# One-instruction seed of 1/sqrt, and a last FFN bank, output included, cut into smaller columns

## The chip, the cores and the metric

The kernel runs on one core of a Trainium2 chip. The metric is the device time of one execution in microseconds (us); each version is executed several times and the median is compared. The engines are named as in the profile: PE (TensorE, matmul), DVE (VectorE), ACT (ScalarE), POOL (GpSimd), SP (SyncE, which here issues most DMAs).

## The reference, cut to what matters

Two transformer-like blocks run one after the other on 256 tokens of width 1024, all in float32: first RWKV mixing, block attention, cross attention and a mixture of 32 experts, then retention with pooling, a SwiGLU feed-forward layer (FFN), a convolution layer and a second FFN. The change touches the norm that stands ahead of every layer and the very end:

```python
def rms_norm(x, g):
    x32 = x.astype(jnp.float32)
    y = x32 * lax.rsqrt(jnp.mean(x32 * x32, axis=-1, keepdims=True) + EPS)
    return (y * g).astype(x.dtype)
...
    h = h + swiglu(rms_norm(h, ffn_norm_g[layer]), ffn_w_gate[layer], ffn_w_up[layer], ffn_w_down[layer])
return rms_norm(h, final_norm_g)
```

## The kernel before, in words

Tokens lie on the 128 partitions in two groups, `tt` = 0 (tokens 0 to 127) and `tt` = 1 (tokens 128 to 255); the residual stream `x` is a tile of 128 x 2 x 1024. Where a row of 1024 columns is made by matmuls it goes to two PSUM banks of 512 columns, `c` = 0 and 1, so that `py[c][tt]` are four banks. A float32 product is made as three matmuls of split operands (lines 467 to 469 of `out_rows`): high by high, low by high, high by low.

`rsqrt` (line 223) makes 1/sqrt(x) on DVE without a table: an integer shift right by one (line 226), an integer multiply by -1 and add of a constant (line 227), which together are the well known seed, then three Newton steps. For at most two columns a step is lines 235 and 238 on one column each, with -x/2 made once (line 231). Fifteen calls are made in the whole kernel: in the norms, in the head norms of RWKV and retention, in the router and in the convolution layer.

`ffn(1)` is the last layer. It leaves its last two chunks of the down projection to `last`, as two functions: `before(c, tt)` adds the second to last chunk to bank `py[c][tt]` (six matmuls of 512 columns), `products(c, tt)` the last one (six more).

`last` (line 287) ends the kernel. `add(c, tt)` issues the last products, adds the bank to `x` (DVE, line 2299), squares and sums the half row (ACT, line 2301, an ACTIVATE and the read of its accumulator into `ss`) and multiplies by the gain (POOL, line 2303) for the halves that need it. `store(tt)` adds the two partial sums (line 2307), calls `rsqrt`, scales the two halves and sends each to DRAM with a DMA of 256 KB (line 2318): for `tt` = 1 the first half is scaled by DVE (line 2314) and sent from SP's queue, the second by ACT (line 2312) and sent from ACT's own queue.

In a `manual_schedule` block each engine runs its instructions in the order in which the code issues them. `last` is such a block, with this order:

```python
with self.tc.manual_schedule(engines={PE, ACT, DVE, POOL}):
    before(0, 0)
    before(1, 0)
    before(0, 1)
    add(0, 0)
    add(1, 0)
    store(0)
    before(1, 1)
    add(0, 1)
    add(1, 1)
    store(1)
```

Elsewhere, outside such blocks, a planner with a model of costs sets each engine's order when the kernel is built. So the splitting of weights (`wlo`, line 323, on DVE) can come to stand between two steps of an `rsqrt`.

Of the kernel before, what the change touches and what calls it, by code (L numbers as in the profile page):

```python
# [10 lines left out]
I32 = mybir.dt.int32  # L11
AF = mybir.ActivationFunctionType
OP = mybir.AluOpType
# [150 lines left out]
class Block:  # L164
# [37 lines left out]
    def vectors(self, pool, first, last):  # L202
        self.vec_at, b = VEC[first][0], VEC[last][1]
        self.vec = pool.tile([128, b - self.vec_at], F32, name="vec", tag="vec")
        return self.vec, self.i["vec"][:, self.vec_at:b]
# [17 lines left out]
    def rsqrt(self, out, x):  # L223
        nc = self.nc
        tmp = self.small(x.shape[-1], name="rs")
        nc.vector.tensor_scalar(out.bitcast(I32), x.bitcast(I32), 1, None, op0=OP.logical_shift_right)
        nc.vector.tensor_scalar(out.bitcast(I32), out.bitcast(I32), -1.0, float(0x5f3759df),
                                op0=OP.mult, op1=OP.add)
        if x.shape[-1] <= 2:
            half = self.small(2, name="rx")[:, 0:x.shape[-1]]  # L230
            nc.vector.tensor_scalar(half, x, -0.5, None, op0=OP.mult)
            for _ in range(3):
                for n in range(x.shape[-1]):
                    t, y = tmp[:, n:n + 1], out[:, n:n + 1]
                    nc.vector.scalar_tensor_tensor(t, y, y, half[:, n:n + 1], op0=OP.mult, op1=OP.mult)
                for n in range(x.shape[-1]):
                    t, y = tmp[:, n:n + 1], out[:, n:n + 1]
                    nc.vector.scalar_tensor_tensor(y, t, 1.5, y, op0=OP.add, op1=OP.mult)
            return
        for _ in range(3):  # L240
            nc.vector.tensor_tensor(tmp, out, out, op=OP.mult)
            nc.vector.scalar_tensor_tensor(tmp, tmp, -0.5, x, op0=OP.mult, op1=OP.mult)
            nc.vector.scalar_tensor_tensor(out, tmp, 1.5, out, op0=OP.add, op1=OP.mult)
# [896 lines left out]
    def cross(self):  # L1140
        nc, i, c = self.nc, self.i, self.c
        self.marks = [self.loads[n].ins for n in (-6, -4)]
        last, end = self.los[-3].ins, self.los[-1].ins
        with self.tc.issue_after(self.loads[-4].ins):
            gm, gx = self.gains(i["mem_norm"], i["norm_xattn"])
# [25 lines left out]

        with self.tc.manual_schedule(engines={PE, ACT, DVE, POOL}):
            rs = self.rstd(m, after=last)
            with self.tc.issue_after(end):
                self.scaled(m, rs, gm, m)
# [732 lines left out]
    def ffn(self, layer, beside=iter(())):  # L1908

        nc, i = self.nc, self.i  # L1910
        wg, wu, wd = [i[n][layer] for n in ("ffn_w_gate_2", "ffn_w_up_2", "ffn_w_down_2")]
        gain, = self.gains(i["ffn_norm_g_2"][layer])
        cut = lambda w, f: w[:, f * 256:(f + 1) * 256].rearrange("(k p) c -> p k c", p=128)
        h, p0, w1, rs = self.enter(gain, cut(wg, 0), cut(wu, 0), self.t9 if layer else self.tx, self.tx)
        r = self.gr.tile([128, 256], F32, name="r", tag="r")
        rb = r[:, None].to_broadcast([128, 2, 256])
        py = [[self.bank(f"f{tt}{c}", self.py) for tt in range(2)] for c in range(2)]
        n = FF // 256
        half = lambda c: slice(c * 512, (c + 1) * 512)
        rows = lambda f: self.weights(wd[f * 256:(f + 1) * 256].rearrange("(k p) c -> p k c", p=128))  # L1920
        cols = lambda w, f: self.weights(cut(w, f))

        def total(w, to):
            ps = [self.bank("f2").rearrange("p (m t) -> p m t", m=2) for _ in range(2)]
            self.out_cols2(w, ps)
            for cb in range(2):
                nc.scalar.activation(to[:, cb], ps[cb][:, 0], AF.Copy)
                nc.vector.tensor_tensor(to[:, cb], to[:, cb], ps[cb][:, 1], op=OP.add)

        def down(f, a):  # L1930
            w = rows(f)
            for c in range(2):
                self.out_rows(w, a, py[c], first=(f == 0), last=False, cols=half(c))

        prev = None
        for f in range(n):
            s = self.pr.tile([128, 512], F32, name="fs", tag="pr").rearrange("p (a t) -> p a t", a=2)
            pg = p0
            if f:
                pg = s  # L1940
                total(cols(wg, f), s)
            pu = self.pr.tile([128, 512], F32, name="fu", tag="pr").rearrange("p (a t) -> p a t", a=2)
            total(cols(wu, f) if f else w1, pu)
            if f == 0:
                self.along(rs, r)
            nc.vector.tensor_tensor(s, pg, rb, op=OP.mult)
            nc.scalar.activation(s, s, AF.Silu)  # L1947
            scaled = nc.gpsimd.tensor_tensor(s, s, rb, op=OP.mult)  # L1948
            if f > 1:
                with self.tc.issue_after(scaled.ins):  # L1950
                    next(beside, None)
            nc.vector.tensor_tensor(s, s, pu, op=OP.mult)
            if f < n - 1:
                a = self.ffa.tile([128, 2, 2, 256], F32R, name="fa", tag="fa")
            else:
                a = self.big(F32R, "fa")[:, 0:1024].rearrange("p (m k t) -> p m k t", m=2, k=2)
            self.split(s, a[:, 0], a[:, 1])
            if f == n - 1 and layer:
                w2, a2 = rows(f - 1), prev[1]
            elif prev is not None:  # L1960
                down(*prev)
            prev = (f, (a[:, 0], a[:, 1]))
        w = rows(n - 1)

        def products(c, tt):
            self.out_rows(w, prev[1], py[c], first=False, cols=half(c), tokens=(tt,))

        def before(c, tt):
            self.out_rows(w2, a2, py[c], first=False, last=False, cols=half(c), tokens=(tt,))

        self.left = (before, products, py) if layer else (products, py, False)

    def conv_weights(self):
# [313 lines left out]
    def last(self):  # L2287
        nc, x = self.nc, self.x
        before, products, py = self.left
        g, = self.gains(self.i["final_norm_g_2"])  # L2290
        xg = self.beside("xg").rearrange("p (a d) -> p a d", a=2)
        o = self.big(name="out", room=self.tx).rearrange("p (a d) -> p a d", a=2)
        half = lambda c: slice(c * 512, (c + 1) * 512)
        ss = self.small(4, name="ss").rearrange("p (t c) -> p t c", t=2)

        def add(c, tt):
            xs = x[:, tt, half(c)]
            products(c, tt)
            nc.vector.tensor_tensor(xs, xs, py[c][tt], op=OP.add)
            sq = self.sq.tile([128, 512], F32, name="sq", tag=f"sq{c}")  # L2300
            nc.scalar.activation(sq, xs, AF.Square, scale=1.0 / 32, accum_out=ss[:, tt, c:c + 1])
            if c or not tt:
                nc.gpsimd.tensor_tensor(xg[:, tt, half(c)], xs, g[:, half(c)], op=OP.mult)

        def store(tt):
            ms, rs = self.small(1, name="ms"), self.small(1, name="rstd")
            nc.vector.tensor_scalar(ms, ss[:, tt, 0:1], ss[:, tt, 1:2], 1e-6, op0=OP.add, op1=OP.add)
            self.rsqrt(rs, ms)
            for c in range(2):
                to, xs = o[:, tt, half(c)], xg[:, tt, half(c)]  # L2310
                if c:
                    nc.scalar.activation(to, xs, AF.Copy, scale=rs)
                elif tt:
                    nc.vector.scalar_tensor_tensor(to, x[:, tt, half(c)], rs, g[:, half(c)], op0=OP.mult, op1=OP.mult)
                else:
                    nc.gpsimd.tensor_scalar(to, xs, rs, None, op0=OP.mult)
                queue = nc.scalar if c and tt else nc.sync
                queue.dma_start(out=self.out[tt * 128:(tt + 1) * 128, half(c)], in_=to)

        with self.tc.manual_schedule(engines={PE, ACT, DVE, POOL}):  # L2320
            before(0, 0)
# [4 lines that stand above are left out]
            store(0)  # L2326
            before(1, 1)
            add(0, 1)
            add(1, 1)
            store(1)  # L2330


# [22 lines left out]
```

## Time and profile before

| what | value |
|---|---|
| median of 3 runs | 1380.73 us (1380.12 to 1380.96) |
| the profiled execution's own time | 1378.72 us |
| its span, first to last instruction | 1376.8 us |
| busy: PE, DVE, ACT, POOL | 89%, 56%, 39%, 11% of the span |
| granted TensorE clock, mean | 0.929 of full speed |
| DMA | 360.10 MB, mean 262 GB/s |

The profile records one execution. All times below are counted from the start of its span, which is 1.92 us shorter than the execution's own time; that time is 2.01 us under the median of the runs. "Idle before" is how long an engine stood still ahead of an instruction, with the instruction whose end released it.

### The profile page before, as it was taken

How to read it: one execution, taken by the hardware profiler on the slowest of the kernel's cores; microseconds unless marked ns; L12 is line 12 of the kernel's file. 1: busy time of each engine (PE TensorE's matmuls, PEld its weight loads, DVE VectorE, ACT ScalarE, POOL GpSimd, SP SyncE). 2: the span in 40 equal slices, each digit the busy share in tenths (PEclk: the TensorE clock that was granted, in tenths of full speed). 3: DMA queues.
4: the chain of work that ended last, by engine and by line, in shares of the span. 5: the costliest groups of instructions: out<-in, count | busy, mean ns of one | idle time of the engine just before them, and what ended most of it. 6: DMA issues, size and time to landing. Idle time of an engine off the chain costs nothing.

```text
span 1376.8 us, 28610 instructions
## 1 busy us (share of the span) xinstructions
PE 1230.7 (89%) x12204; PEld 1023.2 (74%) x12204; DVE 769.3 (56%) x1559; ACT 539.6 (39%) x884; POOL 147.0 (11%) x124
## 2 busy tenths in 40 slices
PE   8999999999886777676767699999999999999997
PEld 7989888898765455444535499788888997888886
DVE  5577547876332132131212386877776789766665
ACT  4553533554221111121111274354555535555553
POOL 1022201002000000000000032012221200111112
PEclk9999989999997877888868799999999999999999
DMA  7535513996999999999999998365556268665520
GB/s 213 184 115 158 159 40 128 356 411 253 385 417 416 418 418 420 418 419 418 419 419 418 381 301 292 102 230 184 184 192 190 78 162 266 207 195 195 191 77 31
DMA packets 146455, 360.10 MB, mean 262 GB/s; under 512 B 6672, under 2 KB 101904, under 8 KB 121744
## 3 DMA queue, kind: packets, MB, share of 16 engines
q1 hardware_dynamic: 144800, 353.69, 69.5%
q0 software_dynamic: 1376, 4.25, 1.0%
q8 instruction: 97, 1.59, 0.5%
q14 instruction: 38, 0.31, 0.1%
q10 hardware_dynamic: 144, 0.26, 0.0%
HBM read 354.92 MB, written 3.26 MB: 260 GB/s over the span
## 4 chain that ended last, share of the span: by engine, by line
PE 41%; DMA 24%; DVE 3%; ACT 1%; issue 0%; SPq 0%; ACTq 0%; DVEq 0%
PE f L445 11%; DMA raw<-in_w_exp_down_dram 10%; DMA raw<-in_w_exp_gate_dram 7%; DMA raw<-in_w_exp_up_dram 6%; PE f L446 6%; PE f L468 3%; PE f L467 3%; PE f L469 3%; PE cv L2105 2%; PE first L452 1%; PE v L469 1%; PE v L467 1%; PE v L468 1%; PE gu L1576 1%; PE xe L1545 1%; PE r L468 1%
## 5 line engine op out<-in xcount | busy, mean ns | idle before, releaser
L323 DVE TENSOR_TENSOR wlo<-raw,whi 128x1024 fp32r<-128x1024 f32 x231 | 292.4, 1273 | 151.8 <-ACT whi L321 146.5
L321 ACT ACTIVATE whi<-raw 128x1024 fp32r<-128x1024 f32 x238 | 249.9, 1057 | 220.5 <-PE f L445 87.7
L445 PE MATMUL f<-hT,whi 128*128 128x512 f32 x672 | 236.3, 395 | 0.0
L1576 PE MATMUL gu<-raw,xe 128*32 128x128 f32 x4096 | 168.9, 312 | 53.5 <-DMA raw<-in_w_exp_up_dram 33.4
L1576 PEld LDWEIGHTS gu<-raw,xe 128*32 128x32 f32 x4096 | 130.9, 122 | 92.2 <-DMA raw<-in_w_exp_up_dram 43.4
L446 PE MATMUL f<-hT,wlo 128*128 128x256 f32 x672 | 188.4, 280 | 0.0
L445 PEld LDWEIGHTS f<-hT,whi 128*128 128x128 f32 x672 | 126.0, 188 | 29.4
L1600 DVE SCALAR_TENSOR_TENSOR ye<-dn,gs,ye 32x256 fp32r<-32x256 f32 x128 | 61.5, 481 | 134.5 <-ACT ye L1599 133.8
L1599 ACT ACTIVATE ye<-dn,gs 32x256 fp32r<-32x256 f32 x128 | 59.6, 465 | 174.8 <-PE dn L1591 118.3
L446 PEld LDWEIGHTS f<-hT,wlo 128*128 128x128 f32 x672 | 127.0, 189 | 0.8
L1591 PE MATMUL dn<-raw,ht 128*32 128x256 f32 x1024 | 85.1, 460 | 45.3 <-DMA raw<-in_w_exp_down_dram 37.7
L1591 PEld LDWEIGHTS dn<-raw,ht 128*32 128x32 f32 x1024 | 34.2, 124 | 82.2 <-DMA raw<-in_w_exp_down_dram 29.6
L1658 DVE SCALAR_TENSOR_TENSOR hd<-gu,scale,hd 128x128 f32<-128x128 f32 x32 | 11.2, 350 | 106.6 <-ACT hd L1657 106.5
L1657 ACT ACTIVATE hd<-gu,scale 128x128 f32<-128x128 f32 x32 | 11.8, 367 | 149.8 <-PE gu L1576 149.8
L1948 POOL TENSOR_TENSOR fs<-fs,r 128x512 f32<-128x512 f32 x22 | 39.3, 1787 | 290.0 <-ACT fs L1947 290.0
L467 PE MATMUL f<-whi,fa 128*128 128x512 f32 x176 | 69.3, 394 | 0.0
L468 PE MATMUL f<-whi,fa 128*128 128x512 f32 x176 | 69.0, 392 | 0.2 <-DVE fa L342 0.2
L469 PE MATMUL f<-wlo,fa 128*128 128x512 f32 x176 | 68.7, 390 | 0.0
L1545 PEld LDWEIGHTS xe<-oh,xn 128*128 128x128 f32 x256 | 36.8, 231 | 12.9 <-issue 12.1
L1545 PE MATMUL xe<-oh,xn 128*128 128x128 f32 x256 | 39.0, 320 | 6.5 <-PEq L1669 5.7
L429 PE MATMUL gt<-hT,whi 128*128 128x256 f32 x128 | 38.7, 303 | 0.0
L467 PEld LDWEIGHTS f<-whi,fa 128*128 128x128 f32 x176 | 33.1, 188 | 7.6 <-ACT fa L341 0.5
(618 smaller groups left out, 2547.3 us busy)
## 6 DMA issues: line engine op xcount, KB each, us to landing
raw<-in_w_exp_gate_dram SPq DMA_DIRECT2D x64, 1024.0 KB, 19.9
raw<-in_w_exp_up_dram SPq DMA_DIRECT2D x64, 1024.0 KB, 19.9
raw<-in_w_exp_down_dram SPq DMA_DIRECT2D x63, 1024.0 KB, 20.0
raw<-in_ffn_w_gate_dram SPq DMA_DIRECT2D x22, 1024.0 KB, 5.4
raw<-in_ffn_w_up_dram SPq DMA_DIRECT2D x22, 1024.0 KB, 5.3
raw<-in_ffn_w_down_dram SPq DMA_DIRECT2D x22, 1024.0 KB, 4.8
raw<-in_w_in_dram SPq DMA_DIRECT2D x20, 1024.0 KB, 5.3
raw<-in_conv_w_pw_dram SPq DMA_DIRECT2D x12, 1024.0 KB, 5.5
```

The source lines that it names most:

```text
L321: nc.scalar.activation(hi, raw[:, k:k + step], AF.Copy)
L323: self.los.append(eng.tensor_tensor(lo, raw[:, k:k + step], hi.bitcast(F32), op=OP.subtract))
L445: nc.tensor.matmul(ps[cb], lhsT=whi[:, k, s], rhs=self.two[n][:, :, kk], start=f, stop=False)
L446: nc.tensor.matmul(ps[cb][:, 1], lhsT=wlo[:, k, s], rhs=self.two[n][:, 0, kk], start=False, stop=l)
L467: nc.tensor.matmul(ps[tt], lhsT=hi[:, k0 + k, s], rhs=whi[:, k, cols], start=f, stop=False)
L468: nc.tensor.matmul(ps[tt], lhsT=lo[:, k0 + k, s], rhs=whi[:, k, cols], start=False, stop=False)
L469: nc.tensor.matmul(ps[tt], lhsT=hi[:, k0 + k, s], rhs=wlo[:, k, cols], start=False, stop=l)
L1545: nc.tensor.matmul(ps[:, a], lhsT=xn[:, tt, d * 128:(d + 1) * 128], rhs=oh[:, tt].rearrange("p e s -> p (e s)"), start=(tt == 0), stop=(tt ...
L1576: nc.tensor.matmul(pg[quarter(n), at:at + 128], lhsT=xe[:, 4 * kh + k], rhs=w[:, k, n // 2, n % 2], start=(at == kh == k == 0), stop=(at > ...
L1591: nc.tensor.matmul(pd[n % 2][quarter(n), 0:256], lhsT=ht[:, quarter(2 * half + k)], rhs=wd[:, k, n * 256:(n + 1) * 256], start=(half + k = ...
L1599: nc.scalar.activation(hi, part, AF.Copy, scale=gs[q])
L1600: nc.vector.scalar_tensor_tensor(lo, part, gs[q], hi.bitcast(F32), op0=OP.mult, op1=OP.subtract)
```

## The change

Four edits:

- In `rsqrt` the shift and the multiply-add become one instruction: the integer bits times -0.5 plus the same constant. It holds for all fifteen calls.
- The last products, bank `py[1][1]`, are issued in two parts of 256 columns. Part 0 goes on in `py[1][1]`; part 1 starts a fresh bank, `f3`. DVE adds the whole of `py[1][1]` to `x` after part 0, and `f3` to the last 256 columns after part 1.
- The half row's square is also made in two parts. As there are now three partial sums, DVE adds the first two in an instruction of its own, issued between part 0's square and part 1's add.
- The output of the last 128 tokens is scaled and sent in quarters of 256 columns (128 KB): columns 0 and 256 on DVE, 512 and 768 on ACT; the first three are sent from SP's queue, the fourth from ACT's.

```diff
     def rsqrt(self, out, x):
-        nc.vector.tensor_scalar(out.bitcast(I32), x.bitcast(I32), 1, None, op0=OP.logical_shift_right)
-        nc.vector.tensor_scalar(out.bitcast(I32), out.bitcast(I32), -1.0, float(0x5f3759df),
-                                op0=OP.mult, op1=OP.add)
+        nc.vector.tensor_scalar(out.bitcast(I32), x.bitcast(I32), -0.5, float(0x5f3759df), op0=OP.mult, op1=OP.add)
...
-        def products(c, tt):
-            self.out_rows(w, prev[1], py[c], first=False, cols=half(c), tokens=(tt,))
+        def products(c, tt, cut=slice(0, 512), to=None):
+            self.out_rows(w, prev[1], [to, to] if to is not None else py[c], first=cut.start > 0,
+                          cols=slice(c * 512 + cut.start, c * 512 + cut.stop), tokens=(tt,))
...
-        def add(c, tt):
-            xs = x[:, tt, half(c)]
-            products(c, tt)
-            nc.vector.tensor_tensor(xs, xs, py[c][tt], op=OP.add)
+        def add(c, tt, part=None):
+            cut = slice(part * 256, part * 256 + 256) if part is not None else slice(0, 512)
+            at = slice(c * 512 + cut.start, c * 512 + cut.stop)
+            xs = x[:, tt, at]
+            to = self.bank("f3")[:, 0:256] if part else py[c][tt][:, cut]
+            products(c, tt, cut, to)
+            if part == 0:
+                nc.vector.tensor_tensor(x[:, tt, half(c)], x[:, tt, half(c)], py[c][tt], op=OP.add)
+            else:
+                nc.vector.tensor_tensor(xs, xs, to, op=OP.add)
             sq = self.sq.tile([128, 512], F32, name="sq", tag=f"sq{c}")
-            nc.scalar.activation(sq, xs, AF.Square, scale=1.0 / 32, accum_out=ss[:, tt, c:c + 1])
+            n = c + (part or 0)
+            nc.scalar.activation(sq[:, cut], xs, AF.Square, scale=1.0 / 32, accum_out=ss[:, tt, n:n + 1])
+            if part == 0:
+                nc.vector.tensor_tensor(ss[:, tt, 1:2], ss[:, tt, 0:1], ss[:, tt, 1:2], op=OP.add)
             if c or not tt:
-                nc.gpsimd.tensor_tensor(xg[:, tt, half(c)], xs, g[:, half(c)], op=OP.mult)
+                nc.gpsimd.tensor_tensor(xg[:, tt, at], xs, g[:, at], op=OP.mult)
...
             self.rsqrt(rs, ms)
+            if tt:
+                quarters(rs)
+                return
...
+        def quarters(rs):
+            for n, at in enumerate((0, 512, 256, 768)):
+                s = slice(at, at + 256)
+                to = o[:, 1, s]
+                if n % 2:
+                    nc.scalar.activation(to, xg[:, 1, s], AF.Copy, scale=rs)
+                else:
+                    nc.vector.scalar_tensor_tensor(to, x[:, 1, s], rs, g[:, s], op0=OP.mult, op1=OP.mult)
+                queue = nc.scalar if n == 3 else nc.sync
+                queue.dma_start(out=self.out[128:256, s], in_=to)
...
             add(0, 1)
-            add(1, 1)
+            add(1, 1, 0)
+            add(1, 1, 1)
             store(1)
```

## Rows read from the trace of the kernel before

**Rows 1.** The page: busy time with share and instructions of each engine.

```profile
PE 1230.7 (89%) x12204; PEld 1023.2 (74%) x12204; DVE 769.3 (56%) x1559; ACT 539.6 (39%) x884; POOL 147.0 (11%) x124
```

**Rows 2.** Stretches: length, busy us per engine, granted clock, DMA share, GB/s.

```profile
0.00:30.00 30.00, 24.95 (x153) 23.05 (x154) 16.49 (x43) 14.43 (x23) 3.32 (x13) 0.89 0.80 242
...
375.00:434.00 59.00, 43.97 (x768) 30.88 (x768) 19.01 (x58) 13.96 (x31) 0.00 (x0) 0.86 1.01 418
...
900.00:1000.00 100.00, 100.00 (x537) 85.98 (x536) 71.88 (x98) 51.73 (x74) 19.00 (x11) 1.00 0.60 194
```

**Rows 3.** The chain that ended last, two stretches: start, length, what.

```profile
814.10 0.12 PE q L430
...
1364.03 0.24 PE f L469
...
1369.17 0.73 ACT sq L2301 x2
...
1372.02 0.72 ACT out L2312
```

**Rows 4.** Timeline of PE: its last matmul.

```profile
1367.96 0.39 PE L469 MATMUL f<-wlo,fa 128*128 128x512 f32 x1
```

**Rows 5.** Timeline of DVE from the first `store` to the end.

```profile
1366.03 0.15 DVE L226 TENSOR_SCALAR rstd<-ms 128x1 int32<-128x1 int32 x1
1366.21 0.15 DVE L227 TENSOR_SCALAR rstd<-rstd 128x1 int32<-128x1 int32 x1
1366.29 0.15 DVE L231 TENSOR_SCALAR rx<-ms 128x1 f32<-128x1 f32 x1
...
1367.70 1.38 DVE L2299 TENSOR_TENSOR x<-x,f 128x512 f32<-128x512 f32 x2
1369.92 0.21 DVE L2307 TENSOR_SCALAR ms<-ss 128x1 f32<-128x1 f32 x1 [0.85 <-ACT sq L2301]
...
1371.95 0.75 DVE L2314 SCALAR_TENSOR_TENSOR out<-x,rstd,raw 128x512 f32<-128x512 f32 x1
```

**Rows 6.** Groups by line and shape, ACT and DVE: busy us, mean ns, idle before.

```profile
L2081 ACT ACTIVATE csg<-csg,vec 128x256 f32<-128x256 f32 x6 | 2.7, 503 | 19.9 <-DVE csg L2078 19.9
L2022 ACT ACTIVATE csq<-dw 128x256 f32<-128x256 f32 x6 | 2.5, 417 | 0.2
...
L1928 DVE TENSOR_TENSOR fu<-fu,f 128x256 f32<-128x256 f32 x22 | 9.1, 414 | 0.0
L2085 DVE SCALAR_TENSOR_TENSOR ut<-cat,vec,csg 128x256 f32<-128x256 f32 x6 | 2.6, 480 | 0.0
```

**Rows 7.** Timeline: the last two DMA issues, on SP's and ACT's queue.

```profile
1372.73 0.33 SPq L2318 DMA_DIRECT2D out_dram<-out  x1
1372.77 0.37 ACTq L2318 DMA_DIRECT2D out_dram<-out  x1
```

**Rows 8.** DMA issues by tile: KB each, median us from issue to landing.

```profile
away<-ut SPq DMA_DIRECT2D x6, 144.0 KB, 1.9
out_dram<-out SPq DMA_DIRECT2D x3, 256.0 KB, 2.3
...
out_dram<-out ACTq DMA_DIRECT2D x1, 256.0 KB, 2.7
```

**Rows 9.** Timeline of DVE: line 227, first and last of 15 calls.

```profile
9.27 0.17 DVE L227 TENSOR_SCALAR rstd<-rstd 128x2 int32<-128x2 int32 x1
...
1370.36 0.15 DVE L227 TENSOR_SCALAR rstd<-rstd 128x1 int32<-128x1 int32 x1
```

**Rows 10.** Tile `rstd`: one of those that waited for it (us, times).

```profile
  PE tr L509: 3.3, 1
```

**Rows 11.** Timeline of DVE: one planned call, weights between its two seed steps.

```profile
223.78 0.17 DVE L226 TENSOR_SCALAR rs<-var 128x8 int32<-128x8 int32 x1
224.58 1.23 DVE L336 TENSOR_TENSOR wlo<-raw,whi 128x1024 fp32r<-128x1024 f32 x1 [0.63 <-ACT whi L335]
225.73 0.17 DVE L227 TENSOR_SCALAR rs<-rs 128x8 int32<-128x8 int32 x1
```

## What I expect of it, before it is run

> **What bounds the kernel now.** I read the page first [rows 1]: PE is busy for 89% of the span, so a DVE instruction taken out counts only where PE, or the end of the kernel, waits for DVE. Then the stretches [rows 2]. From 375 us to about 800 the DMA engines are full (share 1.01, 418 GB/s) while PE is busy for 43.97 of 59 us: the expert weights set the pace there. In the stretch from 900 to 1000 us PE is busy for 100.00 of 100, and the chain at 814 us runs through PE [rows 3]: PE sets the pace after the experts. Only then the end. PE's last matmul starts at 1367.96 [rows 4], yet the span goes on to 1376.8, and in these 8 us the chain goes ACT, DVE, ACT [rows 3]. So the tail is a chain on DVE and ACT, then a DMA.
>
> The reader is to see one thing in the timeline of DVE [rows 5]. When PE ends, DVE is late: it has just done the first `store`'s 1/sqrt, and its two adds for tokens 128 to 255 run back to back, 1367.70 to 1369.08, the second after its bank is complete. A bank that is complete sooner in its first half is therefore of no use by itself; PE is not what the adds wait for.
>
> **The change part by part.** I count the tail from DVE's instructions, against the profiled execution (1378.72 us, 2.01 under the median of the runs).
>
> *Seed in the first `store`.* One step goes: line 227 starts 0.18 us after line 226 [rows 5] (1366.21 less 1366.03). DVE then goes straight on to the adds, which are ready to run: -0.18 us.
>
> *Bank in two parts, on PE.* Twelve matmuls of 256 columns stand for six of 512. A 256-column one takes a step of 0.12 us in the chain at 814 us, a 512-column one 0.24 [rows 3], so PE ends where it did, at about 1368.35 (1367.96 plus 0.39) [rows 4]. DVE asks for the last part over a microsecond later (below). Cost nothing; without that cover it would be what PE is late by.
>
> *The wait that is added.* Before, DVE's last add ends at 1369.08, ACT's square starts at 1369.17 (0.09 later) and takes 0.73 with its read-out [rows 3], and DVE goes on 0.02 later, at 1369.92 [rows 5]: 0.84 us from add to sum. After, the add of part 0 is as long as the old one (it covers all 512 columns), so it ends where the old last add did, less 0.18. Then comes the instruction that adds two partial sums. It needs part 0's square from ACT, and DVE runs in order, so the add of part 1 queues behind it; for that add ACT's second square waits, and for that the end. A half square takes 0.73 less 0.22, the difference between a scaled copy of 512 columns (0.72) [rows 3] and an ACT instruction of 256 with a per-partition operand (0.503) [rows 6]: 0.51. So after part 0's add: 0.09 + 0.51 + 0.02 to the sum; 0.08 until the next, independent instruction starts (1366.29 less 1366.21, rows 5; the upper bound is a dependent step, 0.18); 0.41 for the add of 256 columns [rows 6]; 0.09 + 0.51 + 0.02 again. That makes 1.73 us for 0.84: +0.89, at most +0.99. The lower bound is the case that the second add isn't held: 0.41 + 0.09 + 0.51 + 0.02 = 1.03, or +0.19. I take +0.89, as the sequence in the code leaves no choice to DVE. The part 1 add would start about 0.70 after 1368.90, at 1369.6, so PE's 1368.35 is covered by 1.2 us. That a bare square of 256 columns takes 0.417 [rows 6], 0.09 under the scaled one, moves nothing, since the read-out is in the 0.73. POOL's product with the gain is cut likewise; no step of the chain comes from POOL.
>
> *Seed in the second `store`.* The same step on the path: -0.18.
>
> *Output in quarters.* Counted from DVE's first scaling, at 1371.95 before [rows 5]. Before: DVE is done at 0.75, the DMAs are issued at 0.78 (SP) and 0.82 (ACT) [rows 7], and the one on ACT's queue takes 2.7 to land [rows 8]: 3.52. After: DVE's two take 0.48 each [rows 6], done at 0.48 and 0.96; ACT starts 0.07 later (1372.02) [rows 3] and with 0.503 each is done at 0.57 and 1.07. SP has three issues where it had one, in the order of columns 0, 512, 256: at 0.51, 0.87 and 1.23, each some 0.36 after the one ahead (0.33 and 0.37) [rows 7]; the third finds its data ready since 0.96, so it waits for SP alone. ACT's own follows at 1.10. The nearest row for a quarter (128 KB, 1 KB per partition) is a store of 144 KB from SP, `away`, which lands in 1.9 us [rows 8]: the last quarter lands at 1.23 + 1.9 = 3.13, ACT's perhaps 0.05 later. I take 3.17: -0.35. Bounds: -0.39 (3.13), 0 if a quarter takes the 2.3 of a half on SP (3.53), +0.41 at the 2.7 of ACT's.
>
> Here the Trainium skill speaks against the cut. "DMA: Bandwidth & Descriptors", section "Anatomy of one DMA", gives a DMA a fixed 2.0 us plus its bytes at 436 GB/s, in a fit for DMAs issued from GpSimd; 128 KB would take an estimated 2.3 us and the -0.35 would become about 0. The 1.9 us of the row is less than this formula's fixed part and its bytes together, so the row stands against the page for this size; what quarters of one output do is in no row here.
>
> *The other thirteen seeds.* Each saves about 0.2 us on DVE; calls run from 9 to 1370 us [rows 9]. Six lie after 375 us, and PE or the DMA stream covers them as the stretches show [rows 2]. Seven lie before. One has a visible waiter on PE, the transposes at the start [rows 10]; but of 0.2 us won there little can be left after the stretch in which the weights' bytes set the pace. Bounds: 0, and 7 x 0.2 = -1.4. I take -0.1, near to nothing, as a single wait of that kind is seen and the full DMA stretch lies behind it.
>
> Sum: -0.18 + 0.89 - 0.18 - 0.35 - 0.1 = +0.08 us. On the profiled execution 1378.8, on the median of the runs 1380.8 us.
>
> **The rivals.** About 0.2%, or 2.8 us, is what a measurement of this kernel can tell from no change.
>
> Faster, by *early seeds that carry through*: all seven savings ahead of 375 us reach the end. For it speaks the wait at the start [rows 10], against it the full DMA stretch [rows 2]. -1.4 for -0.1: +0.18 - 1.4 = -1.2, or 1379.5 us.
>
> Faster, *the part 1 add is not held*: if ACT's partial sum were there when DVE asks, the wait grows by 0.19 and not 0.89. Then the sum is -0.62, 1380.1 us. PE's early end speaks for it [rows 4]; the ACT square, which can't start before the add ends, speaks against.
>
> Slower, *a quarter takes as long to land as a half*: place, the third DMA on SP's queue; price, 1.23 + 2.3 or 2.7 instead of 3.17. The output gains nothing or loses 0.41, so the sum is +0.4 to +0.8, 1381.2 to 1381.5 us. It decides already from a landing time of 1.76 us: above that the two seeds and the quarters no longer pay for the 0.89. For it: the third issue is 0.45 later than the old one. Against it: the 1.9 [rows 8]. The skill's fixed 2.0 us, from the page above, would put the time in this case.
>
> Another order, either way: *the planner places the splits elsewhere*. Outside the written-out blocks it may put a weight split between steps of the 1/sqrt, as at 223.78, where two seed steps lie 1.95 us apart [rows 11]. With one step less the order may come out anew. One split of 1.23 us ahead of an awaited result costs, or gives back, 1.23; three of them are needed to pass 2.8 us: 1384.5 or 1377.1 us. For it: splits do stand in such gaps. Against it: PE's 100.00 of 100 us and the full DMA stream [rows 2], under which most orders come to the same time.
>
> **How the numbers follow.** Forecast 0.42 (own range 1380.3 to 1381.3); early seeds that carry 0.20; the add not held 0.06; quarters no sooner 0.18; planner 0.07 slower and 0.07 faster. The first four make 0.86 and lie from 1379.5 to 1381.5; the three runs shown differ by 0.84 us, so I widen to 1378.8 to 1382.4. Within 0.2%: 0.84 (0.86 less 0.02 for scatter); faster 0.09, slower 0.07. The predicted time is the likeliest case's, 1380.8.
>
> **What would show it.** In the profile of the changed kernel: one DVE instruction on line 226 and none on the old line 227, fifteen times; between the adds of part 0 and part 1 DVE idle for about 0.6 us, released by ACT's square; from the end of part 0's add to the final sum about 1.7 us; `rsqrt` 0.18 shorter; four DMAs of 128 KB, the last issue some 1.2 us after DVE's first scaling, landing about 1.9 us later. I am wrong on the tail if part 1's add starts right behind part 0's, or if the quarters land after more than 2.2 us; wrong on the rest if PE's last matmul starts over half a microsecond from 1367.96.

## The result, and the profile after

The kernel became slower: 1386.12 us as the median of six runs (1385.07 to 1388.99) beside 1379.69 us for the kernel before (six runs, 1378.40 to 1380.96). The measured ratio is 1.0052, with a 95% interval of 1.0038 to 1.0065 (the two medians alone give 1.0047). That is outside my range and on the side to which I gave 0.07. The profiled execution took 1385.74 us with a span of 1383.8, against 1378.72 and 1376.8 before, so 7.0 us are to be found in the two traces.

The page of the changed kernel shows no new bound; its first lines answer to [rows 1].

```profile
span 1383.8 us, 28621 instructions
PE 1226.1 (89%) x12210; PEld 1018.5 (74%) x12210; DVE 767.5 (55%) x1547; ACT 540.8 (39%) x887; POOL 148.3 (11%) x125
```

PE's share is what it was. So I looked for the place where the two traces part, by the time at which the same matmuls start. The tile views give each group's first and last start; here are three groups before.

```profile
L709 PE MATMUL am<-ar,bT x64: 269/269/320, 107.1 to 110.0; 64*64 64x128 f32 x64
...
L902 PE MATMUL inv<-d,ab x192: 191/194/258, 162.2 to 175.6; 32*32 32x32 f32 x192
...
L787 PE MATMUL st<-vt,ktk x48: 218/218/267, 186.1 to 208.4; 64*64 64x64 f32 x48
```

The same three after the change:

```profile
L707 PE MATMUL am<-ar,bT x64: 269/269/320, 113.0 to 115.8; 64*64 64x128 f32 x64
...
L900 PE MATMUL inv<-d,ab x192: 191/194/258, 169.0 to 182.6; 32*32 32x32 f32 x192
...
L785 PE MATMUL st<-vt,ktk x48: 218/218/268, 192.8 to 215.1; 64*64 64x64 f32 x48
```

From 20 us up to 77 us the changed kernel is ahead by 0.35 us at most. `am` is late by 5.9 us, `inv` by 6.8, `st` by 6.7. After that the distance hardly moves: the first matmul of the experts starts at 357.7 for 351.1, the last one of their `dn` at 796.7 for 790.1, PE's last matmul at 1374.44 for 1367.96 [rows 4]. The stretch in which the DMA engines are full takes nothing of it back: it starts later and is as long as before. Of the 7.0 us, then, about 6.5 are made between 77 and 190 us, and the rest in the last 12 us.

At 77 us stands the 1/sqrt of the key norm, `self.rsqrt(ks[:, 16:32], ks[:, 0:16])`, line 665 of the kernel before, one of the 15 calls. It lies outside the written-out blocks. Set beside each other instruction by instruction, and the seeds themselves left aside, DVE's orders differ first there. Those of the other engines follow: PE's at 82 us, ACT's at 87, SP's and POOL's at 97 and 98. DVE before, timeline from 78 to 91 us:

```profile
78.53 0.17 DVE L227 TENSOR_SCALAR ks<-ks 128x16 int32<-128x16 int32 x1
...
83.38 1.23 DVE L323 TENSOR_TENSOR wlo<-raw,whi 128x1024 fp32r<-128x1024 f32 x1 [2.37 <-ACT whi L321]
84.53 1.28 DVE L675 TENSOR_TENSOR nk<-nk,kn 128x512 f32<-128x512 f32 x2
...
90.72 1.21 DVE L323 TENSOR_TENSOR wlo<-raw,whi 128x1024 fp32r<-128x1024 f32 x1
```

And after:

```profile
84.30 1.49 DVE L673 TENSOR_TENSOR nk<-nk,kn 128x512 f32<-128x512 f32 x2 [3.46 <-PE kn L670]
...
90.71 1.21 DVE L321 TENSOR_TENSOR wlo<-raw,whi 128x1024 fp32r<-128x1024 f32 x1
```

The reader is to see what is missing. Before, DVE splits a piece of weights at 83.38, in the gap ahead of the multiplication that waits for `kn`, and another at 90.72. After, it idles through that gap, and its one split in this stretch is the one at 90.71: one split fewer is done by then. DVE could not have used the gap, for the split's input was late too. A split is made in two halves, ACT's `whi` and then DVE's `wlo`. PE's new order has `kn` four matmuls of `gt` earlier, and the `gt` matmul whose end lets ACT begin now stands behind `kn`. ACT before, and after:

```profile
82.30 1.06 ACT L321 ACTIVATE whi<-raw 128x1024 fp32r<-128x1024 f32 x1 [1.82 <-PE gt L430]
...
85.52 1.06 ACT L319 ACTIVATE whi<-raw 128x1024 fp32r<-128x1024 f32 x1 [5.14 <-PE gt L428]
```

ACT is done at 86.58, and DVE comes to its half at 90.71, behind four multiplications of 1024 columns that now stand ahead of it. In the changed kernel PE gets there at about 89 us. PE's timeline, before:

```profile
91.65 0.39 PE L429 MATMUL u<-hT,whi 128*128 128x256 f32 x1 [0.79 <-ACT whi L321]
...
134.56 0.39 PE L431 MATMUL u<-hT,wlo 128*128 128x256 f32 x1 [0.24 <-DVE wlo L323]
```

After:

```profile
91.98 0.38 PE L429 MATMUL u<-hT,wlo 128*128 128x256 f32 x1 [2.84 <-DVE wlo L321]
...
135.16 0.38 PE L467 MATMUL v<-wlo,hT 128*128 128x256 f32 x1 [2.23 <-DVE wlo L321]
```

Twice PE waits over two microseconds for a split. The waits of the kernel before at these times are 0.79 and 0.24, ahead of other matmuls, as PE's order is another. And behind the first wait it is granted a lower clock. The stretches before, in the columns of [rows 2]:

```profile
88.50:92.00 3.50, 2.71 (x23) 2.46 (x21) 3.50 (x5) 1.73 (x3) 0.00 (x0) 1.00 0.00 0
92.00:96.40 4.40, 4.40 (x33) 3.92 (x32) 2.49 (x6) 3.31 (x8) 0.00 (x0) 1.00 0.73 236
```

After:

```profile
88.50:92.00 3.50, 0.66 (x5) 0.40 (x3) 3.50 (x5) 2.83 (x3) 0.00 (x0) 1.00 0.00 0
92.00:96.40 4.40, 4.40 (x24) 4.40 (x25) 1.94 (x5) 1.11 (x5) 0.00 (x0) 0.61 0.38 113
```

PE is busy for 0.66 of 3.50 us, then runs at 0.61 of its clock: mostly at the lower of its levels, 1.2 and not 2.4 GHz. How much is waiting and how much clock can be read by letting both stretches end at the same matmul, the first of `st`. Before, with PE's columns alone:

```profile
77.00:107.10 30.10, 29.11 (x235) 0.95 0.49 156
107.10:186.10 79.00, 74.44 (x1058) 0.89 0.42 124
```

After:

```profile
77.00:113.00 36.00, 33.10 (x244) 0.87 0.41 125
113.00:192.80 79.80, 72.40 (x1048) 0.91 0.43 125
```

The work is the same, 1293 and 1292 matmuls. PE is idle for 5.56 us before and 10.30 after (109.10 less 103.55, 115.80 less 105.50): +4.7. It is busy for 2.0 us more, which is the same matmuls at a lower clock. These two sizes are of one execution each; the section on why the prediction was wrong sets the other traces beside them.

The tail has its own 0.5 us or so behind PE's last matmul. DVE after, from the first `store`'s last step to the end (before: [rows 5]):

```profile
1373.80 0.68 DVE L2305 TENSOR_TENSOR x<-x,f 128x512 f32<-128x512 f32 x1
1374.40 0.68 DVE L2303 TENSOR_TENSOR x<-x,f 128x512 f32<-128x512 f32 x1
1375.74 0.62 DVE L2310 TENSOR_TENSOR ss<-ss 128x1 f32<-128x1 f32 x1 [0.66 <-ACT sq L2308]
1376.28 0.41 DVE L2305 TENSOR_TENSOR x<-x,f 128x256 f32<-128x256 f32 x1
1377.33 0.21 DVE L2316 TENSOR_SCALAR ms<-ss 128x1 f32<-128x1 f32 x1 [0.64 <-ACT sq L2308]
...
1379.17 0.88 DVE L2337 SCALAR_TENSOR_TENSOR out<-x,rstd,raw 128x256 f32<-128x256 f32 x2
```

From the end of part 0's add (1375.08) to the final sum it is 2.25 us. The add of two numbers per partition takes 0.62 of it. The chain that ended last has no name for that time:

```profile
1375.78 0.51 issue
1376.28 0.42 DVE x L2305
```

"Issue" is time in which the engine waits for nothing that the profile shows. Beside it, on POOL, the product with the gain:

```profile
1375.63 0.71 POOL L2312 TENSOR_TENSOR xg<-x,raw 128x256 f32<-128x256 f32 x1
```

It starts 0.11 us ahead of DVE's small add, and both end together: 1376.34 and 1376.36.

### The profile page after: what moved, and what is told of

Its sections match the earlier page's. It is cut to its first block, busy times and chain, and to the rows that moved or that the text cites. A ratio compares the mean times of both kernels' runs of the same rounds, so it can differ in the third digit from the quotient of the medians.

```text
span 1383.8 us, 28621 instructions
## 1 busy us (share of the span) xinstructions
PE 1226.1 (89%) x12210; PEld 1018.5 (74%) x12210; DVE 767.5 (55%) x1547; ACT 540.8 (39%) x887; POOL 148.3 (11%) x125
## 4 chain that ended last, share of the span: by engine, by line
PE 40%; DMA 23%; DVE 3%; ACT 1%; issue 1%; SPq 0%; ACTq 0%; DVEq 0%
PE f L443 11%; DMA raw<-in_w_exp_down_dram 10%; DMA raw<-in_w_exp_gate_dram 7%; DMA raw<-in_w_exp_up_dram 6%; PE f L444 6%; PE f L466 3%; PE f L465 3%; PE f L467 3%; PE cv L2104 2%; PE first L450 1%; PE v L467 1%; PE v L466 1%; PE v L465 1%; PE gu L1574 1%; PE r L466 1%; PE xe L1543 1%
## 5 line engine op out<-in xcount | busy, mean ns | idle before, releaser
L1574 PE MATMUL gu<-raw,xe 128*32 128x128 f32 x4096 | 165.6, 307 | 57.1 <-DMA raw<-in_w_exp_up_dram 38.1
L1574 PEld LDWEIGHTS gu<-raw,xe 128*32 128x32 f32 x4096 | 127.6, 120 | 94.9 <-DMA raw<-in_w_exp_up_dram 48.5
L465 PE MATMUL f<-whi,fa 128*128 128x512 f32 (+1 forms) x178 | 69.7, 392 | 0.0
L466 PE MATMUL f<-whi,fa 128*128 128x512 f32 (+1 forms) x178 | 69.4, 390 | 0.2 <-DVE fa L340 0.2
L467 PE MATMUL f<-wlo,fa 128*128 128x512 f32 (+1 forms) x178 | 69.1, 388 | 0.0
L1656 DVE SCALAR_TENSOR_TENSOR hd<-gu,scale,hd 128x128 f32<-128x128 f32 x32 | 11.2, 350 | 103.6 <-ACT hd L1655 103.5
L1543 PEld LDWEIGHTS xe<-oh,xn 128*128 128x128 f32 x256 | 32.9, 210 | 12.6 <-issue 11.7
L1543 PE MATMUL xe<-oh,xn 128*128 128x128 f32 x256 | 35.1, 298 | 6.6 <-PEq L1667 5.8
```

Source lines behind the costliest of these rows:

```text
L465: nc.tensor.matmul(ps[tt], lhsT=hi[:, k0 + k, s], rhs=whi[:, k, cols], start=f, stop=False)
L466: nc.tensor.matmul(ps[tt], lhsT=lo[:, k0 + k, s], rhs=whi[:, k, cols], start=False, stop=False)
L467: nc.tensor.matmul(ps[tt], lhsT=hi[:, k0 + k, s], rhs=wlo[:, k, cols], start=False, stop=l)
L1543: nc.tensor.matmul(ps[:, a], lhsT=xn[:, tt, d * 128:(d + 1) * 128], rhs=oh[:, tt].rearrange("p e s -> p (e s)"), start=(tt == 0), stop=(tt ...
L1574: nc.tensor.matmul(pg[quarter(n), at:at + 128], lhsT=xe[:, 4 * kh + k], rhs=w[:, k, n // 2, n % 2], start=(at == kh == k == 0), stop=(at > ...
```

## The experiments

My theory of the 6.5 us, A in the expectations: they come from the shorter seed, through the planner's order. Its rival: they come from the tail's edit, whose instructions might move the order too. Of the tail's 0.62 us the theory, P in the expectations, is that POOL's product holds the small add; its rival, that the add is slow in that place by itself. Ratios are to the kernel before on the same chip. Where a kernel has one time and no ratio, I read only stretches of its trace, since single executions of the kernel before alone lie between 1376.2 and 1384.0 us.

**The seed alone** (`e1_seed_alone`): the kernel before, with the seed of the change in all 15 calls.

> The one-instruction seed in all fifteen calls, the end as before. Theory A (the planner's new order of weight splits around the 1/sqrt of the key norm, at 77 us, costs PE 6.3 us and everything behind is that much later): +6.0 us against the kernel before, the first products of the last bank 6.3 us later and 0.2 to 0.4 won back in the two last calls. Theory B (the loss is made at the end, by the cut bank and the quarters): -0.4 us, no change that can be told.

**The tail alone** (`e2_tail_alone`): the changed kernel with the seed's two instructions back.

> The cut bank and the quarters alone, with the old seed in two instructions. Theory A: the first 1360 us as before; the tail +1.0 us (wait from the last 512-column add to the final sum 0.84 to 2.25 us as in the changed kernel, output 0.2 shorter), so +1 us at most, near what can be told. Theory B: +6 us or more.

The seed alone took 1387.58 us, ratio 1.0063 (1.0046 to 1.0080). The tail alone took 1379.67, ratio 1.0002 (0.9990 to 1.0013), with no instruction out of its old order ahead of the end. The rival falls: the seed carries the whole loss.

**The change without the key norm's call** (`e3_ks_two`):

```
-    def rsqrt(self, out, x):
+    def rsqrt(self, out, x, two=False):
...
+        if two:  # the old two instructions
...
-        self.rsqrt(ks[:, 16:32], ks[:, 0:16])
+        self.rsqrt(ks[:, 16:32], ks[:, 0:16], two=True)
```

> The whole change, but the key norm's 1/sqrt (the call at 77 us, one of fifteen) keeps the old seed in two instructions. Theory A, that this one call decides: +0.5 us (the tail's loss alone), the wait of PE for a weight split at 89 us gone, the matmuls of the last bank where they were before. Rival C (any of the other planned calls, the head norms or the router, do it as well): stays at +3 us or more.

**The key norm's call alone** (`e4_ks_one`): the kernel before, the same switch the other way round, so that this one call has the short seed and 14 keep the old one.

> The kernel before, with the one-instruction seed in the key norm's call alone. Theory A: +6.3 us from one DVE instruction of 0.17 us less. Rival C: less than half of that.

Without that call the change takes 1379.26 us, ratio 0.9998 (0.9989 to 1.0008); that call alone takes 1386.71, ratio 1.0054 (1.0042 to 1.0067). Fourteen of the fifteen calls move nothing that can be measured; the one makes the loss. The trace of the latter shows the changed kernel's two waits again, on PE:

```profile
91.70 0.39 PE L434 MATMUL u<-hT,wlo 128*128 128x256 f32 x1 [2.84 <-DVE wlo L326]
...
135.05 0.39 PE L472 MATMUL v<-wlo,hT 128*128 128x256 f32 x1 [2.23 <-DVE wlo L326]
```

Is it the new instruction, or that there is one fewer? Two kernels part these: one has the new seed and the old count, the other the old seed and a smaller count.

**The key norm's call with a filler** (`e8_filler`): as the one before, and behind the new seed an instruction of the same shape whose result nothing reads.

```
...
+            nc.vector.tensor_scalar(tmp.bitcast(I32), x.bitcast(I32), -1.0, float(0x5f3759df), op0=OP.mult, op1=OP.add)
...
```

> The kernel before with the one-instruction seed in the key norm's call, and in the place of the removed instruction a filler of the same kind that nothing needs (it writes the scratch column that the next step overwrites). With it the planner gives PE, ACT, POOL and SP the same order as in the kernel before. Theory A (the order is the cause): the 6.3 us are gone, 0.0 +- 1.0 us against the kernel before. Rival D (the one-instruction seed itself, its 16 columns or its result, does it): +6 us stay.

**The old seed, one Newton step fewer in the key norm's call** (`e9_two_newton`):

```
-    def rsqrt(self, out, x):
+    def rsqrt(self, out, x, steps=3):
...
-            for _ in range(3):
+            for _ in range(steps):
...
-        self.rsqrt(ks[:, 16:32], ks[:, 0:16])
+        self.rsqrt(ks[:, 16:32], ks[:, 0:16], steps=2)
```

> The kernel before, old seed in two instructions everywhere, but the key norm's call makes two Newton steps and not three (three DVE instructions less; the norm is a little less exact). The planner then gives ACT, POOL and SP the order of the slow kernels, and PE's but for one group moved. Theory A: about +6 us, though DVE has three instructions less. Rival D: 0, or 0.5 less.

The filler gives the loss back: 1379.83 us, ratio 1.0001 (0.9989 to 1.0013). Doing 0.17 us more on DVE makes the kernel about 7 us faster than doing less. Its PE waits 0.79 again and its DVE splits ahead of the multiplication. In its trace ACT, POOL and SP have the order of the kernel before to the end, DVE too but for the filler's place, and PE but for one record among the experts:

```profile
92.21 0.39 PE L433 MATMUL u<-hT,whi 128*128 128x256 f32 x1 [0.79 <-ACT whi L325]
```

```profile
76.78 0.17 DVE L232 TENSOR_SCALAR rs<-ks 128x16 int32<-128x16 int32 x1
...
83.93 1.23 DVE L327 TENSOR_TENSOR wlo<-raw,whi 128x1024 fp32r<-128x1024 f32 x1 [3.53 <-ACT whi L325]
85.07 1.28 DVE L679 TENSOR_TENSOR nk<-nk,kn 128x512 f32<-128x512 f32 x2
```

One Newton step fewer, with the seed untouched, is slow: 1387.17 us, ratio 1.0054 (1.0037 to 1.0071), and PE waits 2.47 us at the same place:

```profile
91.78 0.39 PE L431 MATMUL u<-hT,wlo 128*128 128x256 f32 x1 [2.47 <-DVE wlo L323]
```

So nothing in the seed is slow. Both ways of making this call shorter bring the order in which the split comes late: ACT, POOL and SP run in the order of the kernel with the key norm's call alone, DVE too outside the call, and PE but for three matmuls of `gt` near `kn` and a few records among the experts. This kernel's profiled execution is the quickest of its six (1383.14; the others 1385.78 to 1390.81). In it `st` is late by 4.4 us only, and the wait at 135 us isn't there: the longest for `v` is 0.5. Its end takes 0.9 longer after the last scaling, as one of its output stores takes 3.6 us to land where the longest of the kernel before takes 2.7.

Now the tail, on top of the change without the key norm's call, so that the planner's order is that of before.

**POOL's product later** (`e5_pool_later`): for the cut bank POOL multiplies once, 512 columns, behind part 1's add.

```
-            if c or not tt:
-                nc.gpsimd.tensor_tensor(xg[:, tt, at], xs, g[:, at], op=OP.mult)
+            if (c or not tt) and part != 0:
+                at = half(c)
+                nc.gpsimd.tensor_tensor(xg[:, tt, at], x[:, tt, at], g[:, at], op=OP.mult)
```

> The changed kernel with the old seed in the key norm (order as before), and POOL's product of the last half row in one piece after the add of part 1. Theory P (the add of two partial sums, 0.62 us for one column, is held by POOL working at the same time): it takes 0.2 us, the add of part 1 starts 0.08 after it, and from the end of part 0's add to the final sum it is 1.75 instead of 2.25 us. Rival Q (the 0.62 us is what a one-column add right behind ACT's read-out costs): stays 0.62 and 2.25.

**The partial sum later** (`e6_sum_later`): the instruction that adds the two partial sums moves behind part 1's add.

```
             if part == 0:
...
             else:
                 nc.vector.tensor_tensor(xs, xs, to, op=OP.add)
+            if part == 1:
+                nc.vector.tensor_tensor(ss[:, tt, 1:2], ss[:, tt, 0:1], ss[:, tt, 1:2], op=OP.add)
...
-            if part == 0:
-                nc.vector.tensor_tensor(ss[:, tt, 1:2], ss[:, tt, 0:1], ss[:, tt, 1:2], op=OP.add)
```

> The same, but POOL's product as in the changed kernel, and the add of two partial sums issued behind the add of part 1. Theory W (DVE's wait for ACT's first square is what the cut costs): from the end of part 0's add to the final sum 1.2 us instead of 2.25 (add 0.41, square 0.61, small steps), as DVE's add of part 1 starts at once; unless POOL, which then works beside that add, stretches it as well.

**Both** (`e10_both_later`): the two edits together.

> Bank in two parts, with both the add of the two partial sums and POOL's product behind the add of part 1. From the end of part 0's add to the final sum 1.25 us (1.39 with the sum moved alone, 1.80 with POOL moved alone), still more than the 0.84 of one whole bank, since DVE and not PE is what is late there; first sum of squares to the end of the span 10.7 us. If the cut of the bank could pay, it would be under 0.84.

With POOL later, DVE's small add takes 0.16 and part 1's add follows 0.08 behind its start, as I had priced it:

```profile
1368.26 0.16 DVE L2315 TENSOR_TENSOR ss<-ss 128x1 f32<-128x1 f32 x1 [0.67 <-ACT sq L2313]
1368.34 0.42 DVE L2310 TENSOR_TENSOR x<-x,f 128x256 f32<-128x256 f32 x1
```

So POOL's product held it. With the sum later, the wait from the last 512-column add to the final sum is 1.39 us; I had expected 1.2, but the small add still meets a product of POOL's and still takes 0.62. With both it is 1.99 where I had expected 1.25, a miss that shows the mechanism best. DVE:

```profile
1367.43 1.22 DVE L2312 TENSOR_TENSOR ss<-ss 128x1 f32<-128x1 f32 x1
1368.76 0.21 DVE L2322 TENSOR_SCALAR ms<-ss 128x1 f32<-128x1 f32 x1
```

POOL:

```profile
1367.38 1.26 POOL L2318 TENSOR_TENSOR xg<-x,raw 128x512 f32<-128x512 f32 x1
```

POOL's product is now twice as wide and starts 0.05 ahead of the small add; the small add takes 1.22 and ends at 1368.65, POOL at 1368.64.

**The seeds without the key norm's, bank whole, output whole** (`e11_seed_not_ks`): the kernel before with the short seed in 14 calls, so the old tail.

> The old end, the one-instruction seed in all calls but the key norm's. First sum of squares to the end of the span 10.75 us as in the run with the seed alone (the second add then waits 0.2 for PE); beside the run with quarters, the difference is what the quarters bring, 0.2 us.

**The same with the output in quarters** (`e7_quarters_alone`): the bank isn't cut. The edit is against the changed kernel:

```
...
-            nc.vector.tensor_scalar(ms, ss[:, tt, tt:tt + 1], ss[:, tt, tt + 1:tt + 2], 1e-6, op0=OP.add, op1=OP.add)
+            nc.vector.tensor_scalar(ms, ss[:, tt, 0:1], ss[:, tt, 1:2], 1e-6, op0=OP.add, op1=OP.add)
...
-            add(1, 1, 0)
-            add(1, 1, 1)
+            add(1, 1)
```

> Seed in one instruction in all calls but the key norm's, the last bank whole as before, the output of the last 128 tokens in quarters. Theory A with what the end showed: the wait of 0.84 us from add to sum is back, quarters give 0.2, two seeds up to 0.36: from the first sum of squares at the end (line 2307 in the kernel before) to the end of the span 10.5 us where the kernel before has 11.0 and the changed one 11.7; in time -0.5 us, too little to be told. If it is told as slower, theory A has missed a call.

The tail of all of these, in us. The first column runs from the start of the first `store`'s sum (line 2307 before) to the end of the span. The others are its parts: to the end of the last add of 512 columns; from there to the final sum; from that to DVE's first scaling of the last output; from there to the end. The end of the span is taken to a hundredth (1376.75 before, 1383.77 after).

| kernel | sum to end | to last 512-column add | to final sum | to first scaling | to the end |
|---|---|---|---|---|---|
| before | 10.97 | 3.30 | 0.84 | 2.03 | 4.80 |
| after | 11.69 | 3.00 | 2.25 | 1.84 | 4.60 |
| seed alone | 10.79 | 3.30 | 0.84 | 1.85 | 4.80 |
| tail alone | 12.08 | 3.19 | 2.25 | 2.03 | 4.61 |
| change without key norm's call | 11.71 | 3.01 | 2.25 | 1.84 | 4.61 |
| POOL's product later | 11.27 | 3.01 | 1.80 | 1.85 | 4.61 |
| partial sum later | 10.85 | 3.01 | 1.39 | 1.85 | 4.61 |
| both later | 11.45 | 3.00 | 1.99 | 1.84 | 4.61 |
| seeds, old tail | 10.79 | 3.30 | 0.85 | 1.84 | 4.80 |
| seeds, quarters, bank whole | 10.60 | 3.31 | 0.85 | 1.84 | 4.61 |

The last one has the shortest tail, and it was timed: 1379.00 us, ratio 0.9996 (0.9985 to 1.0006). It beats the changed kernel, whose ratio was 1.0052, by giving up the two things that cost, but cannot be told from the kernel before: 0.37 us of tail are a fortieth of a per cent, and the interval is 0.2% wide. The cut of the bank pays in none of the forms tried: its best tail is 10.85 us, with the sum moved, where the whole bank with quarters has 10.60.

## Why the prediction was wrong

**The step that failed is the planner's rival, and with it the term for the other thirteen seeds, which I took as -0.1.** I had the mechanism, "the planner places the splits elsewhere", and priced it at one split's own time, 1.23 us, so that "three of them are needed to pass 2.8 us", and I gave it 0.07 on the slow side. Its price and its cover were wrong. My own sign of being wrong on the rest came true: PE's last matmul starts at 1374.44 and not within half a microsecond of 1367.96.

- *The price.* PE's wait for a split is not the split's duration. ACT's half, DVE's half and the multiplications queued between them stand in line: PE waited 2.84 for 0.79 at 92 us and 2.23 for 0.24 at 135 us, +4.0 together, +4.7 in all idle time up to `st`. And the order moved on PE and ACT as well as on DVE. The clock adds +2.0 of busy time in these two executions, which I didn't price at all.
- *The cover.* That "most orders come to the same time" rested on PE's 100.00 of 100 us and on the full DMA stream [rows 2]. Both rows are from behind 375 us. The place lies ahead of it: between 77 and 186 us the DMA engines' share is 0.44 and PE has idle time that an order can lengthen. A full stream doesn't absorb what comes before it either: here it began 6.6 us later and ended 6.6 us later. I had read those two stretches for the thirteen seeds as a whole and not the stretch of each.
- *The sign.* I took the thirteen seeds as 0 to -1.4 us. Twelve of them fit that as far as can be told: without the key norm's call the change can't be told from before (0.9998). One was +6.5. That a shorter call can cost is what the filler and the Newton step show from both sides.

The early seeds that carry through (-1.2 us) can be neither shown nor excluded: the intervals here are over 2.5 us wide. "Not held" did not come: part 1's add is held, as I had argued from the order of the code. Nor did quarters that land as late as halves: 1.9 us on SP's queue for 2.3.

**The tail, by its terms.** I had +0.18 (-0.18, +0.89, -0.18, -0.35); the table has +0.72, counted from the first sum, which comes 6.30 us later than before; from PE's last matmul, 6.48 later, it is 0.54.

- *Seeds.* The second is -0.19, as priced. The first counts only beside the cut bank: with the old tail it is lost again, as the seed alone shows on DVE,

```profile
1375.14 0.69 DVE L2297 TENSOR_TENSOR x<-x,f 128x512 f32<-128x512 f32 x1 [0.21 <-PE f L467]
```

  where the second add, free earlier, waits 0.21 us for its bank. I had said that PE is not what the adds wait for. It was, by a tenth: before, the two adds take 1.38 us together [rows 5], with the cut bank 1.28 (1373.80 to 1375.08). The table has it too, 3.30 to 3.19 without the seed and 3.00 with it. So the bank's cut was worth 0.1 us that I had at nothing; PE's extra matmuls cost nothing, as I said.
- *The wait that is added.* The form was right: part 1's add queues behind the partial sum, which waits for ACT (0.66 idle on DVE; I had 0.62). The size was not: +1.41 (0.84 to 2.25) for +0.89. The 0.5 us between them is the small add, which I took at a step of 0.08 and which ends only with POOL's product. "No step of the chain comes from POOL" is the sentence that was wrong; POOL later gives 0.45 of it back.
- *Quarters.* -0.20 with the cut bank (4.80 to 4.60), -0.19 with the whole one (10.79 to 10.60, 4.80 to 4.61), for -0.35. The landing was near the price, the issues were not. The DMA issues of the changed kernel, with KB each and median us to landing:

```profile
out_dram<-out SPq DMA_DIRECT2D x3, 128.0 KB, 1.9
out_dram<-out ACTq DMA_DIRECT2D x1, 128.0 KB, 2.2
```

  and the DMAs of the tile `out_dram`, with shortest, median and longest issue and first and last start:

```profile
L2339 SPq DMA_DIRECT2D out_dram<-out x3: 332/382/401, 1379.7 to 1380.6; - x3
```

  SP's first issue starts at 0.51 after the first scaling (1379.68 less 1379.17), as priced, but the third at about 1.4 and not 1.23: they start some 0.45 apart, where I had 0.36. With 1.4 for 1.23 my own sum gives 1.4 + 1.9 = 3.3 us for the old 3.5, which is the 0.2 that was measured. The Trainium skill, "DMA: Bandwidth & Descriptors", section "Anatomy of one DMA", whose fit is for DMAs issued from GpSimd, would have put a quarter at an estimated 2.3 us; the trace has 1.9 as SP's median and 2.2 on ACT's queue, so that page was nearer for the latter and my row for the former.

That a two-operand instruction of DVE's waits for POOL is in the Trainium skill, "SBUF — State Buffer", section "Who interferes with whom": a DVE instruction with two inputs in SBUF and a GpSimd one that reads SBUF take turns, and the one that starts first keeps the other out until it is done. The trace agrees with it in the runs of this tail: 0.16 us alone, 0.62 beside a product that had started just before, 1.22 beside one of twice the width. I had looked for a rule on the output's cut and for none on POOL's.

**What stays open.** The split of the 6.7 us at `st` into waiting (4.7) and clock (2.0) is read from one execution of each kernel; no run here changes the one without the other. The other traces share it out differently. From 77 us to the first `st` PE is idle for 5.6 to 7.0 us in the nine kernels with the old order at this place, and for 9.5 to 10.3 in the changed kernel, the seed alone and the key norm's call alone; it is busy for 99.5 to 103.6 us in the nine and for 105.5 to 106.5 in the three. By the medians that is 3.4 us of waiting and 3.7 of clock. The kernel with one Newton step fewer has 8.0 and 105.6. The profiled execution before is the least idle and the most busy of the nine, so the pair above gives the wait too much. Why the planner's model picks this order for the shorter call, I did not look into: only that it does, for two different ways of making the call shorter, and not when the count is restored. The filler has the new seed with the old order, the Newton step the old seed with nearly all of the new one, and the time goes with the order both times. No kernel here has the call one instruction shorter with the old order written out by hand, so that the order alone is the cause is not shown by holding it fixed; nor is it shown which engine's part of the new order makes the loss.

## What to carry to other kernels

Where a planner sets part of the order, set the new instruction order beside the old one before pricing anything: a removed 0.17 us in an unpinned place cost 6.5 us here, and the price of a displaced producer is its consumer's whole new wait, with the clock after it. Look up the cover of an edit in its own stretch of time, call by call, and don't take a full stream that comes later as cover. Cutting work so that a second engine can start earlier pays only if the pieces don't queue behind a join: put the instruction that joins partial results behind all pieces, and look at what another engine does in that very moment.

## What the runs showed of the hardware that I had not expected

An add of 128x1 in SBUF on DVE ends with the POOL multiplication beside it, however short it is by itself: 0.16 us alone, 0.62 beside a product of 256 columns, 1.22 beside one of 512. It hit the kernel before, too. On DVE, at 71 us:

```profile
71.13 1.98 DVE L649 TENSOR_TENSOR fm<-ep,fm 128x12 f32<-128x12 f32 x1
```

On POOL:

```profile
70.69 2.39 POOL L679 TENSOR_TENSOR kp<-kp,kT 128x1024 f32<-128x1024 f32 x1 [1.48 <-DVE kp L678]
```

Twelve columns take 1.98 us and end at 73.11, POOL's at 73.08. DVE's adds of `x` with a bank are not held: those of 1373.80 and 1374.40 above take 0.68 each, the second of them wholly beside POOL's scaling of the first output (from 1374.07, 1.57 us). So a short instruction of DVE's with a long time, beside a busy POOL, is the sign to look for.
